# The first modulation's columns as TensorE products in four column groups, and the opening in a new written order

## The chip, the cores and the metric

The kernel runs on one core of a Trainium2 chip. The metric is device time in microseconds (us), the median of several executions. One execution is profiled as well. Engines are named as in the profile: PE is TensorE's matmul row and PEld its weight loads, DVE is VectorE, ACT is ScalarE, POOL is GpSimd, SP is SyncE, which issues most of the DMAs.

## The reference

One layer of a diffusion backbone over 1024 latent tokens of 1024 channels, with 256 context tokens. What matters here is its beginning: a conditioning vector gives six modulation vectors by one matrix product, the first two of which shift and scale the normed tokens, and the tokens then go through one wide input projection.

```
c_silu = silu(c);  cctx_silu = silu(c_ctx)
sh1, sc1, g1, sh2, sc2, g2 = split(c_silu @ w_ada + b_ada, 6)
csh1, csc1, ...            = split(cctx_silu @ w_ada + b_ada, 6)
hx = rmsnorm(x, norm1_g)   * (1 + sc1)  + sh1
hc = rmsnorm(ctx, norm1_g) * (1 + csc1) + csh1
xq, xk, xv, ... = split(hx @ w_in, offsets)
cq, ck, cv, ... = split(hc @ w_in, offsets)
```

Neighbourhood attention, retention, a merge, and a gated MLP with a depthwise convolution follow. Neither kernel differs from the other in those.

## The kernel before

Tokens are held transposed: channels on the 128 partitions, in eight channel blocks kb of 128, tokens along the free axis, in halves of 512 for the latent grid and one piece of 256 for the context. Each 32-bit product is made of three products of a high part and a low part (`mm3`, L123 to L125; `chain`, L112 to L114): high with high, high with low, low with high. The high part is a rounded copy made on ACT, the low part what is left, subtracted on DVE.

The opening is one block of code under a manual schedule: the order in which the lines are written is the order of each engine's instructions, and each engine takes its own in that order. SP's queue of loads is ordered in the same way, and a load whose buffer is still read holds all loads behind it. The opening's steps are small functions:

- `load_x`, `square_x`, `rstd_x`, `scale_x` (L161, L164, L168 and L169, L172): a block of 128 token rows (eight of the grid, tb 0 to 7, two of the context, 8 and 9) is loaded, squared with a sum on ACT, its root taken on POOL, and its rows scaled on DVE.
- `transp` (L199): PE turns a 128x128 piece of a scaled block into a PSUM bank; eight for each block, 80 in all. The banks have three tags, tp, c0 and c1, with two, three and three buffers, which are all eight banks. `evac_t` (L207) copies a full bank to SBUF on ACT or DVE; where it isn't called, the modulation reads the bank.
- `mod_h` (L219) on ACT gives the modulated high part, `mod_v` (L223) on DVE the same in full precision, `mod_l` (L228) on DVE the low part. `ctx_h`, `ctx_v`, `ctx_l` are the same for the context.
- `load_first`, `split_hi`, `split_lo` (L325, L328): the first pair's q, k, v weights and their two parts. `first_mm(half, kb)`: nine products of 512 columns that add channel block kb to q, k and v of one half of the tokens; sixteen calls in all.
- The shift and scale columns come in two ways. For channel blocks 0 to 3 (`NPE = 2` groups of two blocks), `ag_mm` (L265) multiplies on PE: the vector piece of 128 channels is the stationary operand, 32 columns wide, and 512 weight columns stream; four pieces go to four groups of 32 columns of the array, and add up in four strips of one bank. `ag_ev` copies the bank, `ag_tr` (L274) sums the strips and turns them into columns with four small products, `ag_fin` (L280, L281) adds the bias on DVE. For channel blocks 4 to 7 the weights come transposed and the vector is spread over all partitions (`load_bc`, `silu_bc`, cs0 for the latent tokens, cs1 for the context): `ada_stt` (L303) multiplies and sums on DVE, or `ada_prod` (L309) multiplies on POOL and `ada_sum` (L313) sums on ACT; `ada_fin` (L298, L299) adds the bias.
- Row blocks and modulation weights share one tag, `x`, of 14 buffers of 512 KB.

Then the first pair's q, k and v are copied out of PSUM (`ev_hi`, `ev_lo`), the next pair's q weights (`next_load`, `next_hi`, `next_lo`, L592 and L595) are split, and `next_mm` (L112 to L114) and `ctx_mm` run on PE beside it; `decays` (L556 to L561) makes small tables for the retention on ACT. Behind the manual part a scheduler orders the attention of four pairs, with projections as filler work.

Of the kernel before, what the change touches and what calls it, by code (L numbers as in the profile page):

```python
# [16 lines left out]
P = 128  # L17
# [16 lines left out]
NPE = 2  # L34
# [6 lines left out]
def tile_hybrid_layer(ctx, tc: tile.TileContext, io, dbg=None):  # L41
# [112 lines left out]
    xs, xT = {}, {}  # L154
# [39 lines left out]
    def transp(tb, kbs, tags=None):  # L194
        grid, half, i = tb < NTB, tb // 4 % 2 if tb < NTB else 0, tb % 4 if tb < NTB else tb - NTB
        for n, kb in enumerate(kbs):
            if i == 0:
                tps[grid, half, kb] = p_tile(tags[n])
            pe.transpose(tps[grid, half, kb][:, i * P : (i + 1) * P], xs[tb][:, kb * P : (kb + 1) * P], ident)  # L199
# [4 lines left out]
    def evac_t(grid, half, kb, eng):  # L204
        moved.add((grid, half, kb))
        x = xT[grid, kb, half]
        copy[eng](x, tps[grid, half, kb][:, : x.shape[-1]])  # L207


    def turned(grid, half, kb):  # L210
        x = xT[grid, kb, half]
        return x if (grid, half, kb) in moved else tps[grid, half, kb][:, : x.shape[-1]]
# [22 lines left out]
    cs2 = [(s0 if i else csp).tile([P, D], F32, name=f"cs{i}") for i in range(2)]  # L235
    wad = {}
# [9 lines left out]
    def load_bc(i):  # L246
        sync.dma_start(cs2[i], io["cvec"][i : i + 1].to_broadcast([P, D]))

    def silu_bc(i):
        act.activation(cs2[i], cs2[i], AF.Silu)  # L250


    ag, arow, arow_s, acolT = {}, {}, {}, {}

    def load_ag(g, q):
        ag[g, q] = s_tile("x", 14)
        sync.dma_start(ag[g, q], io["w_ada1g"][g, q])

    def ag_mm(g, q):
        if q == 0:  # L260
            arow[g] = p_tile("tp")
        for e in range(2):
            k = 2 * q + e
            c = 32 * (k % 4)
            pe.matmul(arow[g][c : c + 32], ccol[:, k], ag[g, q][:, e * 512 : e * 512 + 512], start=k < 4, stop=k >= 4)  # L265
# [5 lines left out]
    def ag_tr(g):  # L271
        acolT[g] = p_tile("tp")
        for n in range(4):
            pe.matmul(acolT[g][:, 2 * n : 2 * n + 2], arow_s[g][:, n * P : n * P + P], csum, start=True, stop=True)  # L274

    def ag_fin(g):
# [3 lines left out]
        vec.tensor_tensor(t, acolT[g][:, 0:8].rearrange("p (i k s) -> p i k s", i=2, k=2), bb[:, :, kbs].unsqueeze(3).to_broadcast([P, 2, 2, 2]), ALU.add)  # L280
# [4 lines left out]

    def load_ada(kb):
        wad[kb] = [s_tile("x", 14) for _ in range(2)]
        for i in range(2):
            sync.dma_start(wad[kb][i], io["w_ada1"][kb - 2 * NPE, i])


    acol = cpool.tile([P, 2, KB, 2], F32, name="acol")

    def ada_fin(kb, s, eng):
        t = acol[:, s, kb]
        eng = pool if eng == "pool" else vec
        bb = cst["b"][:, 0:16].rearrange("p (i k) -> p i k", i=2)
        eng.tensor_tensor(t, t, bb[:, :, kb], ALU.add)  # L298
        eng.tensor_tensor(t[:, 1:2], t[:, 1:2], cst["g"][:, 0, kb : kb + 1], ALU.mult)  # L299
        (ca if s else cx)[kb] = (t[:, 1:2], t[:, 0:1])  # L300

    def ada_stt(kb, s, i):
        vec.scalar_tensor_tensor(s_tile("aj", 1), wad[kb][i], 1.0, cs2[s], ALU.mult, ALU.mult, accum_out=acol[:, s, kb, i : i + 1])  # L303

    prods = {}

    def ada_prod(kb, s, i):
        prods[kb, s, i] = s_tile("prod", 3)
        pool.tensor_tensor(prods[kb, s, i], wad[kb][i], cs2[s], ALU.mult)  # L309

    def ada_sum(kb, s, i):
        t = prods[kb, s, i]
        act.activation(t, t, AF.Copy, accum_out=acol[:, s, kb, i : i + 1])  # L313
# [6 lines left out]
    def load_first(half):  # L320
        for t in range(3):
            fraw[half, t] = rawload(io["w_qkv"][0, t, half])
# [7 lines left out]
    def first_mm(half, kb):  # L330
        xh, xl = hxs(0, half)(kb), hxs(1, half)(kb)
        if kb == 0:
            ch[half] = [p_tile(f"c{half}") for _ in range(3)]
        for t in range(3):
            wc, c0 = first[t][kb // 4], (kb % 4) * P
            mm3(perm(ch[half][t], 8), wc[:, 0, c0 : c0 + P], wc[:, 1, c0 : c0 + P], xh, xl, kb == 0, kb == KB - 1)
# [202 lines left out]
    def ada_col2(i):  # L539
        w = ada2[i]  # L540
        late(vec.scalar_tensor_tensor(w, w, 1.0, cs2[0], ALU.mult, ALU.mult, accum_out=col[:, 16 + i : 17 + i]))
        if i + 1 < 32:
            ada_load()
# [46 lines left out]
    def next_hi(i):  # L590
        nxt[i] = place if i else wtile()
        act.copy(nxt[i][:, 0], nraw[i])  # L592
# [21 lines left out]
    ch = {}  # L614
    with tc.manual_schedule():
        load_ag(0, 0)
        load_cc()
        load_x(0)
        load_x(1)
        silu_cc()  # L620
        square_x(0)
        rstd_x(0, 1)
        scale_x(0)
        ag_mm(0, 0)
        load_ag(0, 1)
        ag_mm(0, 1)
        transp(0, (2,), ("c0",))
        transp(0, (3,), ("c1",))
        load_x(2)
        load_ag(0, 2)  # L630
        transp(0, (7,), ("tp",))
        square_x(1)
        rstd_x(1, 1)
        load_cols()
        transp(0, (0,), ("c0",))
        transp(0, (4,), ("c1",))
        ag_mm(0, 2)
        load_x(3)
        load_ag(0, 3)
        scale_x(1)  # L640
        one_plus()
        transp(1, (2,), ("c0",))
        square_x(2)
        rstd_x(2, 1)
        scale_x(2)
        transp(1, (7,), ("tp",))
        transp(0, (1,), ("c0",))
        transp(1, (1,), ("c0",))
        transp(0, (5,), ("c1",))
        transp(2, (1,), ("c0",))  # L650
        load_ag(1, 1)
        load_ag(1, 0)
        square_x(3)
        rstd_x(3, 1)
        scale_x(3)
        transp(1, (0,), ("c0",))
        transp(2, (7,), ("tp",))
        transp(1, (4,), ("c1",))
        transp(2, (2,), ("c0",))
        transp(2, (4,), ("c1",))  # L660
        ag_mm(0, 3)
        transp(3, (1,), ("c0",))
        transp(3, (4,), ("c1",))
        transp(1, (5,), ("c1",))
        transp(2, (5,), ("c1",))
        transp(2, (0,), ("c0",))
        transp(3, (5,), ("c1",))
        load_first(0)
        load_ag(1, 2)
        transp(3, (2,), ("c0",))  # L670
        transp(1, (3,), ("c1",))
        transp(3, (7,), ("tp",))
        ag_ev(0, "act")
        ag_tr(0)
        ag_fin(0)
        transp(3, (0,), ("c0",))
        mod_h(True, 0, 0)
        mod_v(True, 0, 0)
        split_hi(0, 0)
        evac_t(True, 0, 7, "act")  # L680
        ag_mm(1, 0)
        ag_mm(1, 1)
        transp(2, (3,), ("c1",))
        transp(3, (3,), ("c1",))
        transp(0, (6,), ("tp",))
        transp(1, (6,), ("tp",))
        transp(2, (6,), ("tp",))
        load_ag(1, 3)
        mod_l(True, 0, 0)
        split_hi(0, 2)  # L690
        split_lo(0, 2)
        evac_t(True, 0, 5, "vec")
        load_x(4)
        ag_mm(1, 2)
        transp(3, (6,), ("tp",))
        ag_mm(1, 3)
        evac_t(True, 0, 4, "act")
        split_hi(0, 1)
        split_lo(0, 0)
        mod_h(True, 0, 1)  # L700
        evac_t(True, 0, 2, "act")
        load_x(5)
        load_x(6)
        square_x(4)
        mod_v(True, 0, 1)
        mod_l(True, 0, 1)
        evac_t(True, 0, 6, "vec")
        split_lo(0, 1)
        first_mm(0, 0)
# [1439 lines left out]
```

## Time and profile before

| | us |
|---|---|
| median of 3 runs | 1754.88 (1753.91 to 1762.69) |
| the profiled execution | 1755.57 |
| its span, first to last instruction | 1753.8 |
| PE busy in the span | 1707.4 (97%) |
| DVE busy | 1318.1 (75%) |
| ACT busy | 846.3 (48%) |
| POOL busy | 542.6 (31%) |
| mean granted clock of PE | 0.992 |

The span is cut into 40 slices on the page; each digit is a busy share in tenths:

```profile
PE   7799999999999999999999999999999999999997
DVE  5978888766677776787664557888999899866655
POOL 2600000003333343055413300244555555111444
PEclk9899999999999999999999999999999999999998
```

The first slice is 44 us long, and so is the second. They hold the opening: PE is below nine tenths there, DVE at nine in the second slice, POOL busy and then idle for long. A busy share is read with care, since matmuls are pipelined.

### The profile page before, as it was taken

How to read it: one execution, taken by the hardware profiler on the slowest of the kernel's cores; microseconds unless marked ns; L12 is line 12 of the kernel's file. 1: busy time of each engine (PE TensorE's matmuls, PEld its weight loads, DVE VectorE, ACT ScalarE, POOL GpSimd, SP SyncE). 2: the span in 40 equal slices, each digit the busy share in tenths (PEclk: the TensorE clock that was granted, in tenths of full speed). 3: DMA queues.
4: the chain of work that ended last, by engine and by line, in shares of the span. 5: the costliest groups of instructions: out<-in, count | busy, mean ns of one | idle time of the engine just before them, and what ended most of it. 6: DMA issues, size and time to landing. Idle time of an engine off the chain costs nothing.

```text
span 1753.8 us, 24617 instructions
## 1 busy us (share of the span) xinstructions
PE 1707.4 (97%) x8270; PEld 1416.1 (81%) x8270; DVE 1318.1 (75%) x2510; ACT 846.3 (48%) x1802; POOL 542.6 (31%) x459
## 2 busy tenths in 40 slices
PE   7799999999999999999999999999999999999997
PEld 4588888888888888888888888878888888888886
DVE  5978888766677776787664557888999899866655
ACT  6666666653343434543344323634444444554443
POOL 2600000003333343055413300244555555111444
PEclk9899999999999999999999999999999999999998
DMA  9143334442342322677668643723223332586753
GB/s 373 45 123 126 106 105 143 135 146 85 92 130 77 103 62 87 191 243 244 202 195 303 217 154 133 266 86 118 91 90 112 117 103 90 184 286 194 243 171 147
DMA packets 158143, 268.20 MB, mean 153 GB/s; under 512 B 26080, under 2 KB 46784, under 8 KB 158016
## 3 DMA queue, kind: packets, MB, share of 16 engines
q1 hardware_dynamic: 140096, 245.65, 42.7%
q10 hardware_dynamic: 17920, 20.98, 3.4%
q8 instruction: 65, 1.06, 0.3%
q14 instruction: 62, 0.51, 0.1%
HBM read 192.32 MB, written 71.61 MB: 150 GB/s over the span
## 4 chain that ended last, share of the span: by engine, by line
PE 38%; issue 7%; DVE 6%; DMA 3%; POOL 3%; ACT 2%; SPq 0%; ACTq 0%; POOLq 0%; DVEq 0%
PE u L1414 23%; PE y L1414 4%; PE pr L114 2%; PE pr L112 2%; PE pr L113 2%; PE om L125 1%; PE om L124 1%; PE om L123 1%; DVE wc L1440 1%; DMA raw<-d_orr 1%; PE pn L114 1%; PE pn L112 1%; PE pn L113 1%; DMA uu<-d_t 1%; DMA vo<-d_h 1%
## 5 line engine op out<-in xcount | busy, mean ns | idle before, releaser
L1414 PE MATMUL u<-T,wc 128*128 128x512 f32 x960 | 227.5, 393 | 3.8 <-ACT pu L1460 2.6
L1414 PEld LDWEIGHTS u<-T,wc 128*128 128x128 f32 x960 | 180.5, 189 | 45.1 <-ACT pu L1460 6.3
L1414 PE MATMUL y<-wc,ahl 128*128 128x512 f32 x924 | 212.2, 392 | 2.0 <-DVE wc L89 1.8
L1414 PEld LDWEIGHTS y<-wc,ahl 128*128 128x128 f32 x924 | 174.5, 189 | 39.4 <-DVE wc L89 2.5
L113 PE MATMUL mm<-low,wc 128*128 128x512 f32 (+1 forms) x328 | 124.5, 380 | 0.0
L1414 PE MATMUL u<-h2a,wc 128*128 128x512 f32 x480 | 112.4, 390 | 0.7 <-DVE pu L1469 0.7
L112 PE MATMUL mm<-hx,wc 128*128 128x512 f32 x264 | 107.0, 405 | 0.3 <-DVE vc L223 0.3
L89 DVE TENSOR_TENSOR wc<-ur,wc 128x512 fp32r<-128x512 f32 x77 | 60.8, 793 | 61.1 <-ACT wc L88 61.1
L1414 PEld LDWEIGHTS u<-h2a,wc 128*128 128x128 f32 x480 | 90.0, 188 | 19.9 <-DVE pu L1469 1.2
L114 PE MATMUL mm<-hx,wc 128*128 128x512 f32 x264 | 106.0, 402 | 0.0
L1439 ACT CAST wc<-s 128x512 fp32r<-128x512 f32 x80 | 49.6, 622 | 91.0 <-PE u L1414 87.1
L125 PE MATMUL mm<-wc,low 128*128 128x512 f32 (+1 forms) x240 | 91.4, 381 | 0.0
L1414 PE MATMUL u<-hxT,wc 128*128 128x512 f32 x384 | 90.1, 390 | 0.6 <-DVE pu L1469 0.6
L1566 POOL TENSOR_TENSOR col<-col,bcol 128x32 f32<-128x32 f32 x1 | 0.2, 250 | 278.1 <-DVE st L486 278.1
L1440 DVE TENSOR_TENSOR wc<-s,wc 128x512 fp32r<-128x512 f32 x80 | 82.9, 1037 | 3.7 <-ACT wc L1439 3.4
L88 ACT CAST wc<-ur 128x512 fp32r<-128x512 f32 x77 | 47.7, 620 | 77.9 <-PE y L1414 73.0
L1414 PEld LDWEIGHTS u<-hxT,wc 128*128 128x128 f32 x384 | 71.9, 188 | 16.4 <-issue 1.6
L89 DVE TENSOR_TENSOR wc<-raw,wc 128x512 fp32r<-128x512 f32 x93 | 63.2, 687 | 19.3 <-ACT wc L88 18.8
L88 ACT CAST wc<-raw 128x512 fp32r<-128x512 f32 x93 | 57.2, 620 | 39.5 <-DMA raw<-in_w_pret 7.6
L123 PE MATMUL mm<-wc,hx 128*128 128x512 f32 x192 | 75.3, 392 | 0.6 <-ACT r L1115 0.6
L124 PE MATMUL mm<-wc,hx 128*128 128x512 f32 x192 | 75.2, 392 | 0.0
L1440 DVE TENSOR_TENSOR wc<-wr,wc 128x512 fp32r<-128x512 f32 x55 | 55.6, 1018 | 19.0 <-ACT wc L1439 17.0
(400 smaller groups left out, 4755.7 us busy)
## 6 DMA issues: line engine op xcount, KB each, us to landing
ur<-in_w_up SPq DMA_DIRECT2D x80, 256.0 KB
ur<-d_a SPq DMA_DIRECT2D x77, 256.0 KB
aw<-in_w_ada SPq DMA_DIRECT2D x32, 512.0 KB
pj<-in_w_down SPq DMA_DIRECT2D x44, 256.0 KB
d_w<-pj SPq DMA_DIRECT2D x44, 256.0 KB
d_a<-sa SPq DMA_DIRECT2D x44, 256.0 KB
ur<-d_w SPq DMA_DIRECT2D x44, 256.0 KB
d_a<-at SPq DMA_DIRECT2D x33, 256.0 KB
```

Of the source, the lines that this page charges most:

```text
L88: act.copy(hi, src)
L89: (lo_eng or vec).tensor_tensor(lo, src, hi.bitcast(F32), ALU.subtract)
L112: pe.matmul(out, wh, xh, start=k == 0, stop=False)
L113: pe.matmul(out, wh, xl, start=False, stop=False)
L114: pe.matmul(out, wl, xh, start=False, stop=k == n - 1)
L123: pe.matmul(out, ah, bh, start=first, stop=False)
L124: pe.matmul(out, ah, bl, start=False, stop=False)
L125: pe.matmul(out, al, bh, start=False, stop=last)
L1414: pe.matmul(out, a, b, start=first and n == 0, stop=last and n == 2, skip_group_check=True)
L1439: pin(act.copy(w[:, 0], a))
L1440: pin(vec.tensor_tensor(w[:, 1], a, w[:, 0].bitcast(F32), ALU.subtract))
L1566: pool.tensor_tensor(col[:, 16:48], col[:, 16:48], bcol[:, 16:48], ALU.add)
```

## The change

`NPE` goes from 2 to 4: all eight channel blocks get their columns from PE, and `ada_stt`, `ada_prod`, `ada_sum`, `ada_fin`, cs1 and the transposed weights are gone. cs0, which the second modulation still needs later, is loaded and put through silu at the end of the opening. `ag_mm` is called for four channel pieces at once, so all four column groups of the array run side by side, and the order in which its two halves come is free; the strips are summed into the same bank that held them.

```diff
-NPE = 2
+NPE = 4
...
-    def ag_mm(g, q):
-        if q == 0:
-            arow[g] = p_tile("tp")
-        for e in range(2):
-            k = 2 * q + e
-            c = 32 * (k % 4)
-            pe.matmul(arow[g][c : c + 32], ccol[:, k], ag[g, q][:, e * 512 : e * 512 + 512], start=k < 4, stop=k >= 4)
+    def ag_mm(g, r, tag):
+        first = g not in arow
+        if first:
+            arow[g] = p_tile(tag)
+        for k in range(4 * r, 4 * r + 4):
+            c, w = 32 * (k % 4), ag[g, k // 2][:, k % 2 * 512 : k % 2 * 512 + 512]
+            pe.matmul(arow[g][c : c + 32], ccol[:, k], w, start=first, stop=not first)
...
-    def ada_stt(kb, s, i):
-        vec.scalar_tensor_tensor(s_tile("aj", 1), wad[kb][i], 1.0, cs2[s], ALU.mult, ALU.mult, accum_out=acol[:, s, kb, i : i + 1])
...
-    def ada_prod(kb, s, i):
-        prods[kb, s, i] = s_tile("prod", 3)
-        pool.tensor_tensor(prods[kb, s, i], wad[kb][i], cs2[s], ALU.mult)
-
-    def ada_sum(kb, s, i):
-        t = prods[kb, s, i]
-        act.activation(t, t, AF.Copy, accum_out=acol[:, s, kb, i : i + 1])
```

The tag `x` has 19 buffers instead of 14. Two context pieces share one PSUM bank, each bank is filled in any order of blocks, and every piece is copied out by `evac_t` before it is modulated. `first_mm` may take channel blocks in any order. The next pair's first q weight goes to a place in the attention's own memory (`nxt`, which lies where PT will be) instead of a wc buffer.

```diff
-        xs[tb] = s_tile("x", 14)
+        xs[tb] = s_tile("x", NX)
...
+    def bank(grid, half, kb):
+        return (grid, half, kb if grid else kb // 2)
...
-        nxt[i] = place if i else wtile()
+        nxt[i] = place if i else first_next
```

The written order of the opening, some 300 lines, is new. Its last part reads:

```diff
+        first_mm(1, 3)
         next_load(0)
...
+        next_load(1)
+        load_bc()
+        load_ex()
+        silu_bc()
+        for h in range(RH):
+            decays(h)
         dec_scale()
...
+        next_hi(0)
+        next_lo(0)
+        next_hi(1)
+        next_lo(1)
         pairs.append(Pair(0))
         ev_hi(1, 0, 0)
```

Three places show what moves. The first is the start of SP's queue, before the change: `in_x` and `in_ctx` are token rows, `in_w_ada1g` the modulation weights for PE, `ccol` the conditioning vectors.

```order
L257 DMA x<-in_w_ada1g 128x1024
L240 DMA ccol<-in_ccol 128x8x2
L161 DMA x<-in_x 128x1024 x2
L257 DMA x<-in_w_ada1g 128x1024
L161 DMA x<-in_x 128x1024
L257 DMA x<-in_w_ada1g 128x1024
L74 DMA bcol<-in_bcol 128x48
```

And with the change:

```order
L161 DMA x<-in_x 128x1024
L161 DMA x<-in_ctx 128x1024
L161 DMA x<-in_x 128x1024 x3
L161 DMA x<-in_ctx 128x1024
L161 DMA x<-in_x 128x1024 x4
L247 DMA ccol<-in_ccol 128x8x2
L265 DMA x<-in_w_ada1g 128x1024 x4
L93 DMA raw<-in_w_qkv 128x512
L265 DMA x<-in_w_ada1g 128x1024
```

All ten blocks of token rows, the context's two among them, now stand ahead of the vectors and of every weight.

The second place is PE up to its first product for q, k and v, which is the first row of L123; `ident` is a transpose, `ccol` a modulation product, `csum` a sum of strips. Before:

```order
L199 MATMUL tp<-ident,x 128x128
L274 MATMUL tp<-csum,arow 128x2 x4
L199 MATMUL c_204<-ident,x 128x128
L265 MATMUL tp<-x,ccol 32x512 x4
L199 MATMUL c_188<-ident,x 128x128 x2
L199 MATMUL tp<-ident,x 128x128 x3
L265 MATMUL tp<-x,ccol 32x512 x2
L199 MATMUL tp<-ident,x 128x128
L265 MATMUL tp<-x,ccol 32x512 x2
L123 MATMUL c_319<-hx_123,wc 128x8x8x8
```

And with the change:

```order
L203 MATMUL c_376<-ident,x 128x128 x3
L203 MATMUL c_327<-ident,x 128x128
L273 MATMUL tp<-x,ccol 32x512 x4
L203 MATMUL tp<-ident,x 128x128 x2
L273 MATMUL tp<-x,ccol 32x512 x4
L281 MATMUL tp<-csum,arow 128x2 x4
L203 MATMUL c_322<-ident,x 128x128
L123 MATMUL c_461<-hx_123,wc 128x8x8x8
```

Before, 32 of the 80 transposes and the sums of group 0 alone stood ahead of that product; now all 80 transposes and the sums of group 1 do.

The third place is DVE in the middle of the opening: `vh` is a modulated piece, `low` a low part, `wc` a weight, `aj` a column sum. Before:

```order
L303 SCALAR_TENSOR_TENSOR aj,acol<-x,cs_152 128x1024
L228 TENSOR_TENSOR low<-vh,hx_129 128x512
L228 TENSOR_TENSOR low<-vh,hx_133 128x512
L223 TENSOR_SCALAR vh<-low,acol 128x512
L228 TENSOR_TENSOR low<-vh,hx_137 128x512
L223 TENSOR_SCALAR vh<-low,acol 128x512
L328 TENSOR_TENSOR wc<-raw,wc 128x512 x2
L228 TENSOR_TENSOR low<-vh,hx_107 128x512
L303 SCALAR_TENSOR_TENSOR aj,acol<-x,cs_152 128x1024
```

And with the change, from the columns of group 1 on:

```order
L287 TENSOR_TENSOR acol<-tp,bcol 128x2x2x2
L288 TENSOR_TENSOR acol<-acol,gcol 128x2x2
L231 TENSOR_SCALAR vh<-low,acol 128x512
L236 TENSOR_TENSOR low<-vh,hx_127 128x512
L231 TENSOR_SCALAR vh<-low,acol 128x512
L231 TENSOR_SCALAR vc<-low,acol 128x256
L236 TENSOR_TENSOR low<-vh,hx_129 128x512
L231 TENSOR_SCALAR vh<-low,acol 128x512 x2
L236 TENSOR_TENSOR low<-vh,hx_135 128x512
```

The column sums are gone from DVE, and the context's pieces (`vc`) stand among the grid's instead of at the end. Behind the opening the instructions of every engine are the same, in the same order.

More of the change, by code (lines that the diff above doesn't have):

```diff
@@ L192, in tile_hybrid_layer, with transp, turns @@
     tps = {}
[L194 to L199, printed above, removed]
+    def bank(grid, half, kb):
+        return (grid, half, kb if grid else kb // 2)
+    def transp(tb, kb, tag):
+        grid = tb < NTB
+        key = bank(grid, tb // 4 if grid else 0, kb)
+        if key not in tps:
+            tps[key] = p_tile(tag)
+        c0 = tb % 4 * P if grid else kb % 2 * C + (tb - NTB) * P
+        pe.transpose(tps[key][:, c0 : c0 + P], xs[tb][:, kb * P : (kb + 1) * P], ident)
+    def turns(grid, half, kb):
+        t = tps[bank(grid, half, kb)]
+        return t if grid else t[:, kb % 2 * C : kb % 2 * C + C]
     copy = {"act": act.copy, "vec": vec.tensor_copy}
@@ L234, in tile_hybrid_layer @@
     csum = s0.tile([P, 2], F32, name="csum")
-    cs2 = [(s0 if i else csp).tile([P, D], F32, name=f"cs{i}") for i in range(2)]
-    wad = {}
+    cs2 = csp.tile([P, D], F32, name="cs")
     def load_cc():
@@ L271, in ag_tr @@
     def ag_tr(g):
-        acolT[g] = p_tile("tp")
         for n in range(4):
-            pe.matmul(acolT[g][:, 2 * n : 2 * n + 2], arow_s[g][:, n * P : n * P + P], csum, start=True, stop=True)
+            pe.matmul(arow[g][:, 2 * n : 2 * n + 2], arow_s[g][:, n * P : n * P + P], csum, start=True, stop=True)
     def ag_fin(g):
@@ L318, in tile_hybrid_layer, with load_f @@
     fraw = {}
-    def load_first(half):
-        for t in range(3):
-            fraw[half, t] = rawload(io["w_qkv"][0, t, half])
+    def load_f(half, t):
+        fraw[half, t] = rawload(io["w_qkv"][0, t, half])
     def split_hi(half, t):
@@ new lines, in tile_hybrid_layer @@
+        evac_t(False, 0, 5, "act")
+        load_ag(0, 1)
+        transp(9, 1, "c0")
+        load_ag(0, 3)
+        silu_cc()
+        transp(8, 0, "c0")
+        square_x(4)
+        transp(3, 5, "c0")
+        transp(3, 2, "c1")
+        transp(3, 0, "tp")
+        transp(2, 4, "c1")
+        transp(0, 1, "c0")
+        load_f(0, 1)
+        rstd_x(4, 1)
+        transp(8, 7, "c1")
+        transp(9, 0, "c0")
+        transp(8, 6, "c1")
+        transp(2, 1, "c0")
+        evac_t(True, 0, 3, "act")
@@ L917, in tile_hybrid_layer @@
-        ctx_l(5)
-        ctx_h(6)
-        ctx_l(6)
+        ag_tr(3)
+        split_lo(1, 2)
+        mod_h(True, 1, 4)
+        mod_l(True, 0, 5)
+        mod_h(True, 1, 5)
+        first_mm(0, 4)
+        ag_fin(3)
+        ctx_v(7)
+        ctx_h(7)
+        mod_v(True, 0, 7)
+        mod_v(True, 0, 6)
+        mod_v(True, 1, 7)
+        ctx_v(6)
+        mod_h(True, 0, 6)
+        ctx_l(7)
+        mod_h(True, 0, 7)
+        mod_l(True, 0, 6)
+        mod_l(True, 0, 7)
+        mod_h(True, 1, 7)
@@ new lines, in tile_hybrid_layer @@
+        first_mm(0, 5)
+        first_mm(0, 6)
+        mod_l(True, 1, 7)
+        mod_v(True, 1, 5)
+        mod_h(True, 1, 6)
+        ctx_v(5)
+        first_mm(0, 7)
+        mod_l(True, 1, 5)
+        mod_v(True, 1, 4)
+        ctx_h(6)
+        mod_v(True, 1, 6)
+        first_mm(1, 7)
+        ctx_l(5)
+        mod_l(True, 1, 6)
+        first_mm(1, 5)
+        first_mm(1, 1)
+        ctx_h(4)
+        mod_l(True, 1, 4)
+        ctx_l(6)
+        first_mm(1, 6)
+        first_mm(1, 4)
+        first_mm(1, 0)
@@ L2063, in layout @@
     out["ccol"] = ac(out["cvec"].reshape(2, KB, P).transpose(2, 1, 0))
-    out["w_ada1"] = ac(w_ada[:, :2048].T.reshape(2, KB, P, D).transpose(1, 0, 2, 3)[2 * NPE :])
     out["w_ada2"] = ac(w_ada[:, 2048:].T.reshape(32, P, D))
```

541 lines of the change are left out of this document (230 added, 311 removed).

## The prediction

> **What bounds the kernel now.** I read the page first, then the windows before and after the point where the change ends, then PE's and DVE's instructions in order of time. The columns of a window are its length, the busy time of PE, PEld, DVE, ACT and POOL with counts, the granted clock, the DMA share and GB/s.
>
> ```profile
> 0.00:84.19 84.19, 61.70 (x273) 42.43 (x273) 61.86 (x87) 52.66 (x105) 37.18 (x44) 0.92 0.57 214
> 84.19:1753.80 1669.61, 1645.69 (x7998) 1373.69 (x7998) 1256.24 (x2424) 793.67 (x1698) 505.42 (x416) 1.00 0.46 150
> ...
> 40.00:60.00 20.00, 14.78 (x54) 11.28 (x53) 18.81 (x19) 11.75 (x20) 14.95 (x13) 0.83 0.31 115
> 60.00:80.00 20.00, 13.14 (x52) 10.39 (x52) 19.53 (x29) 13.60 (x36) 10.67 (x6) 0.83 0.00 1
> ```
>
> At 84.19 us PE takes the first product of the next pair. From there PE is busy 98.6% of the time; before it, 73%. Between 40 and 80 DVE is the full engine (38.3 of 40 us), PE has 12 us free, and DMA is nearly idle from 60 on. So the opening waits for DVE, the rest for PE, and only the opening is edited.
>
> ```profile
> 48.67 0.79 PE L124 MATMUL c<-low,wc 128*128 128x512 f32 x1 [3.65 <-DVE low L228]
> ...
> 75.97 0.47 PE L199 MATMUL tp<-ident,x 128*128 128x128 f32 x1 [4.85 <-DVE vc L223]
> ...
> 84.19 0.47 PE L112 MATMUL mm<-hx,wc 128*128 128x512 f32 x1 [0.32 <-DVE vc L223]
> ...
> 95.77 0.36 PE L112 MATMUL mm<-hc,wc 128*128 128x256 f32 x1 [0.44 <-DVE qS L421]
> ```
>
> Every long wait of PE is for DVE. Why DVE is full is seen at one place: three POOL products and two row scalings of DVE begin together.
>
> ```profile
> 53.67 7.94 POOL L309 TENSOR_TENSOR prod<-x,cs 128x1024 f32<-128x1024 f32 x3
> ...
> 53.74 5.66 DVE L172 TENSOR_SCALAR x<-x,rstd 128x1024 f32<-128x1024 f32 x2 [0.86 <-POOL rstd L169]
> ...
> 29.30 0.74 DVE L172 TENSOR_SCALAR x<-x,rstd 128x1024 f32<-128x1024 f32 x1
> ```
>
> The scaling takes 0.74 us with POOL idle, and 2.83 us each beside the products. So the column sums on POOL cost DVE time too.
>
> **What goes.** The groups of instructions in the first 100 us name it:
>
> ```profile
> L309 POOL TENSOR_TENSOR prod<-x,cs 128x1024 f32<-128x1024 f32 x8 | 21.7, 2723 | 7.6 <-ACT prod L313 6.4 <-DMA x<-in_w_ada 1.1
> ...
> L303 DVE SCALAR_TENSOR_TENSOR aj<-x,cs 128x1024 f32<-128x1024 f32 x8 | 11.4, 1426 | 0.0
> ...
> L313 ACT ACTIVATE prod<-prod 128x1024 f32<-128x1024 f32 x8 | 8.4, 1055 | 0.9 <-POOL prod L309 0.9
> ```
>
> All three end: 11.4 us of DVE, 8.4 of ACT, 21.7 of POOL, with the stretching of DVE beside POOL. The weight bytes stay: eight 512 KB tiles for eight.
>
> **What comes, on PE.** Two more groups of four columns each.
>
> ```profile
> 16.98 1.09 PE L199 MATMUL c<-ident,x 128*128 128x128 f32 x8
> ...
> 19.23 1.07 PE L265 MATMUL tp<-x,ccol 128*32 128x512 f32 x8
> ...
> 27.44 0.95 PE L274 MATMUL tp<-csum,arow 128*128 128x2 f32 x8
> ...
> 79.72 0.39 PE L124 MATMUL c<-low,wc 128*128 128x512 f32 x1
> 79.94 0.39 PE L125 MATMUL c<-hx,wc 128*128 128x512 f32 x1
> ```
>
> Four products in four column groups (eight records) take 1.07 us, so a group's eight take 2.14, and its column sums 0.95: 3.1 us, twice. A product of 512 columns starts every 0.228 us, so one row block for q, k and v (nine) takes 2.05 us. Eight transposes take 1.09 us.
>
> **When the modulation can start.** All ten row blocks stand ahead of the first weights on SP, so arrival sets the beginning.
>
> ```profile
> 7.45 1.06 ACT L164 ACTIVATE v<-x 128x1024 f32<-128x1024 f32 x1 [0.61 <-DMA x<-in_x]
> ...
> 8.80 1.06 ACT L164 ACTIVATE v<-x 128x1024 f32<-128x1024 f32 x1 [0.20 <-DMA x<-in_x]
> ...
> 20.00:40.00 20.00, 18.19 (x98) 12.95 (x95) 17.10 (x28) 16.65 (x29) 5.25 (x5) 1.00 1.03 404
> ```
>
> 512 KB at 404 GB/s is 1.30 us; the squares that wait for blocks start 1.35 apart. Block 0, now behind one large tile and the small ccol, lands by 7.4; alone in front, a block lands between 4.6 and 6.1 (one or two steps less; I take 4.6, since ccol's many small pieces go too). Then by count: group 0, the 14th large tile, at 4.6 + 13 x 1.30 + 0.8 for ccol = 22.3; group 1, four more tiles, a 256 KB weight and two small loads, at 28.3; group 2 at 36.1; group 3 at 40.7. Before, weights came among the first blocks and blocks 4 to 9 late, so the modulation now starts later, and the part behind it must win that back. The buffers (19 for 14) don't hold SP: the 20th tile waits for block 1, whose last transpose is the 45th of 80, done long before that tile's turn at 30 us.
>
> ```profile
> 16.96 0.59 ACT L269 COPY arow<-tp 128x512 f32<-128x512 f32 x1 [1.74 <-PE tp L265]
> ...
> 24.00 0.50 PE L123 MATMUL c<-hx,wc 128*128 128x512 f32 x1
> ...
> 30.61 0.80 ACT L219 ACTIVATE hx<-low,acol 128x512 fp32r<-128x512 f32 x1
> ...
> 22.40 0.68 DVE L207 COPY low<-c 128x512 f32<-128x512 f32 x1
> ...
> 49.68 0.54 DVE L223 TENSOR_SCALAR vh<-low,acol 128x512 f32<-128x512 f32 x1
> ...
> 64.43 0.68 DVE L228 TENSOR_TENSOR low<-vh,hx 128x512 fp32r<-128x512 f32 x1
> ...
> 84.48 0.42 DVE L223 TENSOR_SCALAR vc<-low,acol 128x256 f32<-128x256 f32 x1
> ```
>
> On PE the first product for q, k, v (24.00 in before) now stands behind all 80 transposes and group 1. Up to group 0 the transposes hide behind the loads: 80 at 0.136 are 10.9 us of PE, in banks that DVE and ACT must empty, 24 copies where there were 12. Group 0 goes from 22.3 over its products (2.1), the copy on ACT (0.6), the sums (0.95) and two small DVE instructions (0.35), with 0.4 of hops, to columns at 26.7. On DVE three modulations (two of 512, one of 256), two subtractions, three copies and two weights' low parts follow: 2 x 0.54 + 0.42 + 0.68 + 0.42 + 3 x 0.68 + 2 x 0.68 = 6.0, so the third weight is ready at 32.7. On PE group 1 has landed at 28.3 and waits for a bank and its place till 29.8 for the second half of its products; copy and sums follow, to 32 or 33. Both say **32.7 for the first product**; I take 31.5 and 35 as bounds, the later one for the first block landing at 6.1 with a copy or two in the way.
>
> **From there PE sets the end.** 16 blocks x 2.05 = 32.8, groups 2 and 3 another 4.3 and their sums 1.9: 39.0 us, **to 71.7**. Does DVE keep up? Group 1's columns are ready at 33.3; from there to the last weight's low part, which the fifth block needs, its column holds eight modulations (0.54) and eight subtractions (0.68) of 512, three of each of 256 (0.42), three low parts (0.68) and two small ones: 14.7 us, or 13 as far as rows start before the last has ended. That is 46.3 to 48. PE comes there after 4 x 2.05 + 4.3 + 1.9 = 14.4 us, at 47.1. So nothing to 1 us is lost. The last eight blocks then take PE 16.4 us and DVE some 7, so DVE is done first. DVE's whole opening adds up to 46 us (10 x 0.74, 8 x 0.68 copies, 6 x 0.68 parts, 16 x 0.54, 16 x 0.68, 16 x 0.42 for the context, 3 us of small ones) where it was 61.86 busy.
>
> The weights of the next pair are what PE takes next. They moved behind all of ACT's modulations:
>
> ```profile
> 31.32 1.05 ACT L250 ACTIVATE cs<-cs 128x1024 f32<-128x1024 f32 x1
> ...
> 60.58 1.28 ACT L556 ACT_TABLE_LOAD   x1
> ...
> 77.85 0.60 ACT L592 CAST wc<-raw 128x512 fp32r<-128x512 f32 x1
> 78.36 0.29 ACT L556 ACTIVATE dec<-ex,lg 128x1 f32<-128x1 f32 x1
> 78.56 0.28 ACT L557 ACTIVATE dec<-ex,lg 128x1 f32<-128x1 f32 x1
> ```
>
> After ACT's last modulation (about 54 on DVE's count) come silu (1.05), the table (1.28), 24 decays 0.19 apart (4.6), two casts (1.2) and DVE's part (0.7): 62 to 64. PE arrives at 72, so 8 us cover it; all exposed it would cost its 8.8. Behind them the evacuations of the first pair queue; a cast for the pair after stands among them and waits for the last use of the first weights, so they mostly run beside the next pair's 11 us of products, as they do now.
>
> **Sum.** With 0.3 of hop and half a microsecond of stall, the next pair starts at 72.5 instead of 84.19: 11.7 less. The 0.44 stall at 95.77 should go, as half the evacuations come earlier: 12.1. Behind it the order is unchanged and PE-bound, so it carries. The profiled execution took 1755.57 (span 1753.8 and 1.77 around it), so 1743.5; the median shown is 0.69 lower, and I forecast **1743**. Bounds: first product 1.2 earlier or 2.3 later, DVE 0 to 4 short: 1740 to 1749.
>
> **Rivals.** *The clock is half at the start of the products.*
>
> ```profile
> 6.90 1.92 PE L265 MATMUL tp<-x,ccol 128*32 128x512 f32 x4 [6.90 <-ACT ccol L244]
> ...
> 15.86 1.05 PE L265 MATMUL tp<-x,ccol 128*32 128x512 f32 x4
> ...
> 48.00:52.00 4.00, 3.33 (x8) 2.66 (x9) 4.00 (x9) 1.51 (x3) 1.15 (x3) 0.51 0.41 133
> ...
> 50.97 0.63 PE L123 MATMUL c<-hx,wc 128*128 128x512 f32 x1
> 51.39 0.63 PE L124 MATMUL c<-low,wc 128*128 128x512 f32 x1
> ```
>
> After 3.65 us of idling the clock is 0.51 and products start 0.43 apart. The first group's four records took 1.92, later ones 1.05. PE now has nothing but transposes for its first 10 us. If they don't wake it, groups 0 and 1 take 2 us more in the chain and the first eight products 1.6: 4 us, 1747. For: the opening rows are slow. Against: between 11.9 and 15.9 transposes stood mixed with products and it woke. Chance 0.15. The Trainium skill, "TensorE: Matmul & The Clock Gate", Part 4: PE-mode transpose, states that transposes don't count as work for the gate; this trace, where the two are mixed, can't decide it.
>
> *DVE stays the bound.* If the searched order makes it wait for ACT at each block, PE goes at DVE's pace: 5 us lost, 1748. Chance 0.14.
>
> *The gain is taken back later*, by loads that now fall together: 1753 to 1755. Only 1.4% of PE's time behind 84.19 is idle. Chance 0.05.
>
> *Slower:* the clock stays half through the products. Each costs 0.20 more; the 12.1 are gone at 60 of the 144, and all 144 give +29, 1772. It needs gaps all along, as DVE made them before; there half clock ended after some 14 products each time. Chance 0.06.
>
> That the column sums stay on DVE is excluded by the order: no such row is left.
>
> **Chances.** Forecast 0.60 (1740 to 1746), the others as given. Within 0.5% (8.8 us, about what can be told from no change) fall two thirds of the first rival, most of the second, and the third: faster 0.71, same 0.23, slower 0.06. The range 1740 to 1749 leaves out the last two rivals.
>
> **What will show it.** Right: no 128x1024 product on POOL or DVE in the first 100 us; scalings all near 0.75; first q, k, v product near 33; next pair near 72 with PE full from 50. Wrong: a clock below 0.9 between 30 and 60 (first rival), waits of PE for low (second), a cast of the next pair as PE's last releaser (ACT's tail uncovered).

## The result, and the profile after

| | before | after |
|---|---|---|
| median of 7 runs each, us | 1755.21 (1752.28 to 1762.69) | 1741.64 (1737.7 to 1745.63) |
| ratio of the two | | 0.9915, 95% interval 0.9892 to 0.9938 |
| the profiled execution | 1755.57 | 1743.48 |
| its span | 1753.8 | 1741.4 |
| first q/k/v product starts | 24.00 | 35.48 |
| next pair's first product starts | 84.19 | 74.16 |
| first context product | 95.77 | 85.30 |

The change makes the kernel 0.85% faster. The windows of the kernel after, cut as those of before were (length, busy time of PE, PEld, DVE, ACT and POOL with counts, granted clock, DMA share, GB/s):

```profile
0.00:74.16 74.16, 57.11 (x320) 42.85 (x321) 46.39 (x94) 52.58 (x105) 16.21 (x33) 1.00 0.69 254
74.16:1741.40 1667.24, 1643.64 (x7999) 1371.83 (x7997) 1250.72 (x2412) 787.64 (x1687) 501.09 (x410) 1.00 0.46 149
40.00:60.00 20.00, 20.00 (x112) 14.59 (x105) 19.01 (x43) 18.11 (x41) 0.00 (x0) 1.00 0.50 172
60.00:80.00 20.00, 20.00 (x90) 16.57 (x89) 8.10 (x12) 9.42 (x22) 4.90 (x5) 1.00 0.27 79
```

Between 40 and 80 us the full engine has changed: PE is busy 40 of 40 us at full clock, where it had 27.9. DVE's busy time up to the next pair has shrunk from 61.86 to 46.39 us. Behind the opening PE is as busy as before (98.6%).

PE's instructions of the opening in order of time (start, length, and in brackets what ended an idle time), the first q/k/v product being L123 and the next pair's L112:

```profile
10.59 0.47 PE L203 MATMUL c<-ident,x 128*128 128x128 f32 x1 [10.59 <-DVE x L172]
14.41 1.76 PE L203 MATMUL c<-ident,x 128*128 128x128 f32 x7 [3.35 <-DVE x L172]
...
19.87 1.15 PE L203 MATMUL c<-ident,x 128*128 128x128 f32 x9
...
22.70 1.06 PE L203 MATMUL c<-ident,x 128*128 128x128 f32 x8 [1.46 <-DVE low L215]
...
24.56 1.92 PE L273 MATMUL tp<-x,ccol 128*32 128x512 f32 x16 [0.25 <-ACT low L215]
...
27.25 0.55 PE L203 MATMUL c<-ident,x 128*128 128x128 f32 x3 [0.51 <-DVE x L172]
...
28.41 0.95 PE L281 MATMUL tp<-csum,arow 128*128 128x2 f32 x8
...
35.48 0.47 PE L123 MATMUL c<-hx,wc 128*128 128x512 f32 x1
...
74.16 0.39 PE L112 MATMUL mm<-hx,nxt 128*128 128x512 f32 x1
...
85.30 0.36 PE L112 MATMUL mm<-hc,wc 128*128 128x256 f32 x1
```

From 35.48 to 74.16 no wait is left. Ahead of it there are two things that the forecast did not have: the transposes from 14.41 to 19.2 us start 0.21 us apart and only then 0.11, and the sums of group 0 (28.41) stand behind transposes that wait for a scaling (27.25). Where that scaling comes from is seen on ACT:

```profile
20.62 0.65 ACT L215 COPY low<-c 128x256 f32<-128x256 f32 x2 [2.87 <-PE c L203]
21.28 1.28 ACT L251 ACT_TABLE_LOAD   x1
22.58 0.42 ACT L251 ACTIVATE ccol<-ccol 128x256 f32<-128x256 f32 x1
22.90 1.04 ACT L164 ACTIVATE v<-x 128x1024 f32<-128x1024 f32 x1
...
54.46 1.05 ACT L257 ACTIVATE cs<-cs 128x1024 f32<-128x1024 f32 x1
55.51 1.28 ACT L535 ACT_TABLE_LOAD   x1
...
61.27 0.60 ACT L571 CAST nxt<-raw 128x512 fp32r<-128x512 f32 x1
```

Block 4's square (22.90) waits in ACT's queue behind copies, the sigmoid table and the SiLU. Its root on POOL follows, block 7's root stands behind that in POOL's queue, and the scalings of blocks 4 and 7 on DVE come last:

```profile
24.98 0.75 DVE L172 TENSOR_SCALAR x<-x,rstd 128x1024 f32<-128x1024 f32 x1 [0.70 <-POOL rstd L169]
26.45 0.75 DVE L172 TENSOR_SCALAR x<-x,rstd 128x1024 f32<-128x1024 f32 x1 [0.71 <-DMA bcol<-in_bcol]
...
29.45 0.17 DVE L287 TENSOR_TENSOR acol<-tp,bcol 128x8 f32<-128x8 f32 x1 [0.92 <-PE tp L281]
29.66 0.17 DVE L288 TENSOR_TENSOR acol<-acol,gcol 128x4 f32<-128x4 f32 x1
```

The columns of group 0 are complete at 29.83. The scaling at 26.45 is put down to a DMA; POOL's root for block 7 is written from 25.86 to 26.41 and fits that start as well.

### The profile page after: what moved, and what is told of

It reads as the page before. It is cut to its first block, busy times and chain, and to the rows that moved or that the text cites. A ratio compares the mean times of both kernels' runs of the same rounds, so it can differ in the third digit from the quotient of the medians.

```text
span 1741.4 us, 24675 instructions
## 1 busy us (share of the span) xinstructions
PE 1700.8 (98%) x8318; PEld 1414.7 (81%) x8318; DVE 1297.1 (74%) x2505; ACT 840.2 (48%) x1791; POOL 517.3 (30%) x443
## 4 chain that ended last, share of the span: by engine, by line
PE 76%; issue 7%; DVE 6%; POOL 4%; DMA 3%; ACT 3%; SPq 0%; POOLq 0%; ACTq 0%; DVEq 0%
PE u L1387 26%; PE y L1387 4%; PE mm L114 4%; PE mm L112 4%; PE mm L113 4%; PE mm L123 3%; PE mm L124 3%; PE mm L125 3%; PE R L496 2%; PE pr L112 2%; PE ptp L478 2%; PE pr L113 2%; PE pr L114 2%; PE om L125 1%; PE om L123 1%
## 5 line engine op out<-in xcount | busy, mean ns | idle before, releaser
L112 PE MATMUL mm<-hx,wc 128*128 128x512 f32 x256 | 103.7, 405 | 0.0
L114 PE MATMUL mm<-hx,wc 128*128 128x512 f32 x256 | 102.8, 402 | 0.0
L123 PE MATMUL mm<-wc,hx 128*128 128x512 f32 x192 | 75.2, 392 | 0.6 <-ACT r L1088 0.6
```

What stands on the lines that cost most here:

```text
L112: pe.matmul(out, wh, xh, start=k == 0, stop=False)
L114: pe.matmul(out, wl, xh, start=False, stop=k == n - 1)
L123: pe.matmul(out, ah, bh, start=first, stop=False)
```

## The experiments

Totals of one kernel spread by some 8 us, which is more than half of the change's own gain, so the opening is judged by its marks: first transpose, first q/k/v product, next pair's first product. The first transpose itself comes between 10.0 and 11.0 us from one execution to the next, so the distance from it is the cleaner number.

| kernel | first transpose | first q/k/v product | distance | next pair | ratio of medians to before, run beside it, 95% interval |
|---|---|---|---|---|---|
| after | 10.59 | 35.48 | 24.89 | 74.16 | 0.9915 (0.9892 to 0.9938) |
| `e1_clear_first` | 10.61 | 35.87 | 25.26 | 74.55 | 0.9903 (0.9887 to 0.9920) |
| `e_nx14` | 10.05 | 35.33 | 25.28 | 74.01 | 0.9915 (0.9896 to 0.9935) |
| `e_warm` | 10.17 | 35.14 | 24.97 | 73.81 | 0.9916 (0.9903 to 0.9928) |
| `e1c_sq4` | 12.06 | 35.80 | 23.74 | 74.48 | 0.9920 (0.9901 to 0.9938) |
| `e_sq4` | 10.94 | 34.54 | 23.60 | 73.22 | 0.9883 (0.9867 to 0.9900) |
| `e_warm_sq4` | 10.96 | 33.13 | 22.17 | 71.81 | 0.9912 (0.9894 to 0.9930) |

The first four have the same chain of work up to the first product apart from one part, and their distances lie within 0.4 us. `e_tail4` and `e_pin_after` below, whose chain up to there is that of the kernel after, have 25.57 and 25.23, so differences of up to 0.7 us mean nothing.

### What the parts of the change are worth

**Columns on PE, old order.** The kernel before with `NPE = 4`; groups 2 and 3 stand where the old order had its sums, and all `ada_` steps are gone.

```diff
-NPE = 2
+NPE = 4
...
-        ada_sum(4, 0, 1)
+        ag_mm(2, 0)
+        ag_mm(2, 1)
...
+        ag_ev(2, "act")
+        ag_tr(2)
+        ag_fin(2)
```

> The kernel before, with all columns as products on PE (NPE = 4) and its old written order: the DVE and POOL column sums are taken out and groups 2 and 3 put where the old order had a first sum and a third block's products. If the columns carry the gain, the first product stays near 24 us, DVE's rows are short everywhere, and PE's first product for the next pair comes at 70 to 76 us (84.19 before, 74.16 with the whole change): 1741 to 1747. If the new order carries it, that product stays at 80 or later: 1751 or more.

Measured: next pair at 80.54, 3.65 us earlier, where the whole change gives 10.03. Median 1745.33, ratio 0.9933 (0.9915 to 0.9951). By the mark, this order keeps about a third of the opening's gain. The totals don't separate this kernel from the one after, since the two intervals overlap; they are taken up below. DVE is no longer full, but the chain of group 3 stands open, as DVE's instructions in order of time show:

```profile
52.06 0.17 DVE L280 TENSOR_TENSOR acol<-tp,bcol 128x8 f32<-128x8 f32 x1 [8.33 <-PE tp L274]
...
55.26 0.69 DVE L228 TENSOR_TENSOR low<-vh,hx 128x512 fp32r<-128x512 f32 x1
```

DVE stands idle for 8.33 us until the sums are there, PE then waits 2.59 us for the low part, and from 50 to 60 us it is busy for 6.04 us at a clock of 0.71. Where the two groups stand was my choice, so this is one old order and not the best one: that a new order was needed at all isn't shown.

**POOL's share alone.** The kernel before with POOL's eight column products and ACT's eight sums done as eight more sums on DVE.

```diff
-        ada_prod(6, 0, 0)
-        ada_sum(6, 0, 0)
+        ada_stt(6, 0, 0)
```

> The kernel before, with the eight column products of POOL (and their sums on ACT) done as eight more sums on DVE. If POOL's products stretch DVE's work by some 14 us, as the rows of before suggest (two scalings in 5.66 us, a low part in 2.63), then DVE pays 8 x 1.2 = 9.8 and saves 14, and the next pair starts near 80 instead of 84.19: 1751. If DVE pays nothing for POOL, DVE has 9.8 us more and the next pair starts near 94: 1765.

The two groups of DVE in the first 90 us (busy time, mean ns of one):

```profile
L303 DVE SCALAR_TENSOR_TENSOR aj<-x,cs 128x1024 f32<-128x1024 f32 x16 | 19.5, 1220 | 0.2
...
L172 DVE TENSOR_SCALAR x<-x,rstd 128x1024 f32<-128x1024 f32 x10 | 7.3, 751 | 13.0 <-POOL rstd L169 13.0
```

DVE's sums grew from 11.4 to 19.5 us, and still its busy time up to the next pair fell from 61.86 to 55.98 and the next pair came at 76.27 instead of 84.19. So POOL's products had cost DVE 14 us (5.9 less plus 8.1 of new sums). Taking them off POOL, and their sums off ACT, moves the next pair by 7.9 us in the old order, where 4 were expected and the whole change gives 10.03. A wait of 1.79 us for DVE then stands ahead of the first context product; the median is 1750.85, ratio 0.996 (0.9943 to 0.9977).

### Why the first product comes at 35.5 and not at 32.7

**The loads.** SyncE waits for POOL's memset of `ccol` before it can issue that load (15.71 us) and the weights behind it (16.44). Here the memset stands first.

```diff
+    def clear_cc():
+        pool.memset(ccol, 0.0)
+
     def load_cc():
-        pool.memset(ccol, 0.0)
...
     with tc.manual_schedule():
+        clear_cc()
         load_x(1)
```

> The changed kernel, with POOL's clearing of ccol moved to the head of POOL's queue, so that SP doesn't wait for it with the loads of all modulation weights (issued at 15.71 us in the changed kernel, after SP had nothing from 6.3 on). If these loads set the first product, it comes at 32.5 to 33 instead of 35.48 and the next pair at 71 to 72 instead of 74.16: 3 us less. If the chain over ACT and POOL sets it (the copies of context pieces at 20.62, the table load, the square of block 4 at 22.90, its root), the first product stays after 34.5.

`ccol` was issued at 7.70 and the weights from 8.96, over 7 us earlier, and nothing moved: distance 25.26. The theory that these loads alone set the first product fell. Fewer buffers point the same way:

```diff
-    xs, xT, NX = {}, {}, 19
+    xs, xT, NX = {}, {}, 14
```

> Kernel after with 14 buffers for row blocks and weights of the modulation instead of 19 (the kernel before had 14 in two pools). Computes the same. The 15th tile (a tile of group 1's weights) then waits until the first row block's last transpose is read, at about 23 us, instead of being issued at about 17. Theory 'the buffers are needed for group 1': group 1's products move from 31.31 to about 33 to 35, the first q/k/v product from 35.48 to 37 to 39, the next pair's first product from 74.16 to 76 to 78, total 2 to 4 us more. Rival 'the loads don't set the opening' (clearing ccol first had brought them 8 us forward and changed nothing): first product and total the same within 0.5 us.

Distance 25.28, next pair at 74.01: the five more buffers of the change are not needed for its gain.

**The half rate of the transposes.** 84 transposes of the identity keep PE busy ahead of the real ones.

```diff
+    wake = p_tile("tp")
+
+    def stir(n):
+        for _ in range(n):
+            pe.transpose(wake[:, 0:P], ident, ident)
...
+        stir(60)
         transp(0, 2, "c1")
+        stir(24)
```

> Kernel after, with 84 transposes of the identity into an unused PSUM tile on TensorE: 60 ahead of the first real transpose and 24 behind it, so that TensorE is busy from about 1.5 us to 14.4 us, where in kernel after it waits. Computes the same. Question: is the late first q/k/v product (35.48 us against the 32.7 forecast) due to the transposes of 14.41 to 19.5 us, which ran at half rate (0.21 us apart instead of 0.11)? Theory 'cold transposes': the real transposes from 14.4 on are 0.11 us apart, about 2.5 us are saved on TensorE's queue, group 0's columns are ready at 27.5 instead of 29.83, the first q/k/v product starts at 33 to 33.5, the next pair's first product at 71.7 to 72.2 instead of 74.16, total 2 to 2.5 us less. Rival 'scalings and copies': TensorE only waits longer for VectorE's scalings and copies; first product 35.0 to 35.5, next pair's first product 73.7 to 74.2, total the same.

Distance 24.97: no change. But the run does not test its theory cleanly, since the clock fell again; PE's instructions and windows show it:

```profile
1.36 8.97 PE L597 MATMUL tp<-ident 128*128 128x128 f32 x60 [1.36 <-POOL ident masks.py:199]
10.17 0.31 PE L203 MATMUL c<-ident,x 128*128 128x128 f32 x1
10.31 2.78 PE L597 MATMUL tp<-ident 128*128 128x128 f32 x24
13.97 0.99 PE L203 MATMUL c<-ident,x 128*128 128x128 f32 x7 [0.87 <-DVE x L172]
15.84 0.33 PE L203 MATMUL tp<-ident,x 128*128 128x128 f32 x1 [0.88 <-DVE x L172]
```

```profile
16.00:19.00 3.00, 3.00 (x16) 2.77 (x16) 2.14 (x6) 1.15 (x2) 1.59 (x3) 0.53 0.72 147
```

The first seven transposes ran at full rate (0.99 us where they had taken 1.76); after two pauses of 0.87 and 0.88 us the clock was 0.53 from 16 to 19 us, and the gain was gone.

**The square of block 4,** first with `ccol` loaded and its SiLU done ahead of everything, so that ACT has no table to load among the copies:

```diff
+        load_cc()
         load_x(1)
+        silu_cc()
         square_x(1)
...
         square_x(7)
+        square_x(4)
...
-        load_cc()
...
-        silu_cc()
...
-        square_x(4)
```

> The changed kernel, with ccol cleared, loaded and put through silu first, and the square of block 4 right behind that of block 7. It frees the loads as the run with the clearing alone does, and also the chain over ACT and POOL. If either of the two sets the first product, it comes at 31.5 to 33 here, and the next pair at 70.5 to 72: 2 to 4 us less than the changed kernel. If neither, it stays at 35.

`ccol` in front delayed all row blocks by 1.5 us (first transpose 12.06), so the first product moved to 35.80; from the first transpose on, 1.15 us were won. Without that load in front, block 4 ahead of block 7 and the memset first:

```diff
+        clear_cc()
         load_x(1)
...
+        square_x(4)
         square_x(7)
...
-        square_x(4)
```

> Kernel after with ccol's clearing at the head of GpSimd's queue and block 4's square ahead of block 7's, and no transposes of the identity: the run with both (first q/k/v product 33.13 us, next pair's first product 71.81) without its first part. Computes the same. Question: which of the two brought the 2.35 us? Theory 'the squares chain': all of it comes from blocks 4 and 7 being scaled at 21.9 instead of 24.98 and 26.45; TensorE's half rate on the transposes is hidden behind the scalings; first q/k/v product 33.1 to 33.8, next pair's first product 71.8 to 72.5. Rival 'both are needed': the transposes at half rate hold the groups' products back by another 1 to 2 us; first product 34.3 to 35.5, next pair's first product 73 to 74.2.

Distance 23.60, 1.3 us less than after, next pair at 73.22. The rival held: this is one half. The scalings of blocks 4 and 7 now follow each other without a wait, and the transposes are still at half rate:

```profile
14.77 1.76 PE L203 MATMUL c<-ident,x 128*128 128x128 f32 x7 [3.35 <-DVE x L172]
...
24.53 1.41 DVE L172 TENSOR_SCALAR x<-x,rstd 128x1024 f32<-128x1024 f32 x2
```

The memset stands first in this run and in the next, so how much the square would have given with the late loads isn't measured. With the transposes of the identity added:

> Kernel after, with the 84 transposes of the identity of the run before, ccol's clearing at the head of GpSimd's queue (so that SyncE doesn't wait for it), and block 4's square ahead of block 7's on ScalarE instead of behind the sigmoid table and the SiLU (22.90 us), so that blocks 4 and 7 are scaled as soon as VectorE comes to them instead of at 24.98 and 26.45. Computes the same. Theory 'three small chains, each hidden behind the others': alone each gives nothing, together the sums of group 0 no longer wait for block 7's transposes, group 0's columns at 26 to 27, first q/k/v product 31.5 to 33, next pair's first product 70.5 to 72, total 2.5 to 3.5 us less than kernel after. Rival 'the copies set it' (ScalarE's and VectorE's copies of the turned blocks, about 12 us of work on each between 18 and 35): first product not before 35, total as kernel after.

```profile
10.96 0.27 PE L203 MATMUL c<-ident,x 128*128 128x128 f32 x1
11.07 2.78 PE L599 MATMUL tp<-ident 128*128 128x128 f32 x24
13.87 0.99 PE L203 MATMUL c<-ident,x 128*128 128x128 f32 x7
15.72 0.33 PE L203 MATMUL tp<-ident,x 128*128 128x128 f32 x1 [0.86 <-DVE x L172]
...
23.17 1.93 PE L275 MATMUL tp<-x,ccol 128*32 128x512 f32 x16
...
33.13 0.47 PE L123 MATMUL c<-hx,wc 128*128 128x512 f32 x1
```

Here only one such pause fell, the clock stayed full, and the real transposes came 0.11 us apart until they ran into the copies. Distance 22.17, another 1.4 us. The two causes together are 2.7 us. The pair with one more wait far behind the opening, below, repeats it: 25.23 in `e_pin_after`, 22.46 in `e_pin_warm_sq4`. The total did not follow: 2.5 to 3.5 us less than the kernel after was expected, and the ratio is 0.9912 against 0.9915.

### The tail on ACT

Each of the 24 exponentials of the decay tables is done four times, 13.4 us more on ACT (72 more, 0.186 apart).

```diff
-        for h in range(RH):
+        for h in list(range(RH)) * 4:
             decays(h)
```

> Kernel after with each of the decay tables' exponentials on ScalarE done four times (24 become 96, each about 0.19 us: some 13.7 us more on ScalarE; the result is the same). Question: what covers the tail that ScalarE has ahead of the next pair's first product? Theory of the prediction (it ends at 63.2, TensorE is full to 74.16: 11 us of cover): casts of the next weights end at about 75.5 and VectorE's low half at 77, so the next pair's first product starts at 76.5 to 78 instead of 74.16, total 2 to 4 us more. Rival 'the tail is on the path': 13 us more on both. Rival 'there is more cover than that' (the next pair's weights are not what that product waits for): 74.2 and no change.

```profile
76.80 0.50 PE L112 MATMUL mm<-hx,nxt 128*128 128x512 f32 x1 [1.48 <-ACT nxt L571]
```

PE's wait is 1.48 us and is put down to the cast of the next pair's weight: the tail was covered by some 12 us (13.4 less 1.48; this is one execution). In the kernel after that cast ended at 61.87, 12.3 us ahead of 74.16. Most of the rest of the 2.64 us by which this mark moved was there at the first product already (36.50 instead of 35.48).

### Why the totals spread

In this part the kernels are unchanged. Between 1100 and 1150 us the profiles differ by some 5 us, and it is one meeting of DVE and POOL. The kernel after, in order of time:

```profile
1125.11 7.60 DVE L89 TENSOR_TENSOR T<-uu,T 128x512 fp32r<-128x512 f32 x7
...
1125.42 1.53 POOL L1402 TENSOR_TENSOR s<-s,ur 128x512 f32<-128x512 f32 x1 [10.54 <-DMA ur<-in_w_up]
...
1126.91 1.75 POOL L1403 TENSOR_TENSOR s<-ur 128x512 f32<-128x512 f32 x1
...
1128.73 1.62 POOL L1404 TENSOR_TENSOR s<-ur,s 128x512 f32<-128x512 f32 x1
```

and `e_nx14`:

```profile
1123.31 4.29 DVE L89 TENSOR_TENSOR T<-uu,T 128x512 fp32r<-128x512 f32 x7
...
1123.56 5.20 POOL L1402 TENSOR_TENSOR s<-s,ur 128x512 f32<-128x512 f32 x1 [10.25 <-DMA ur<-in_w_up]
```

Either three of DVE's low halves take 1.78 us each instead of 0.68, as long as POOL's sums beside them, or POOL's sum waits until DVE's run has ended. In the first case the conv steps behind DVE's run are late and PE stands:

```profile
1120.00:1140.00 20.00, 16.79 (x71) 13.22 (x70) 19.86 (x22) 12.26 (x20) 4.86 (x3) 0.97 0.48 158
1140.00:1150.00 10.00, 10.00 (x41) 8.14 (x40) 7.54 (x8) 2.03 (x4) 9.31 (x6) 0.89 0.41 153
```

(kernel after: 3.2 us idle, then a clock of 0.89), against `e_nx14`:

```profile
1120.00:1140.00 20.00, 19.98 (x89) 16.22 (x88) 19.83 (x24) 11.67 (x19) 13.71 (x6) 1.00 0.52 168
```

Of the eleven profiles without a further edit there, six show the first case (both kernels of the comparison among them) and five the second. The old order with columns on PE had the second, and its offset to before jumps by 5.0 us between 1127 and 1182 us. So of the 13.7 us by which its profile is shorter, 3.65 were there at the next pair and 5.0 come from this meeting; the other 5 built up in small steps on both sides of it and stay unexplained. Which case its three other executions had isn't known, so its median stays open. To take the meeting away, POOL's sum of that unit waits for DVE's last low half; both engines keep their order.

```diff
-            own(eng.tensor_tensor(self.s2, self.s1, self.a11, ALU.subtract))
+            behind(own(eng.tensor_tensor(self.s2, self.s1, self.a11, ALU.subtract)))
...
+        low_of = last_vec()
         conv(j, *us2)
-    units[PLAIN + 1].load()
+    units[PLAIN + 1].load(behind=lambda ins: after_vec(ins, low_of))
```

> Kernel before, with one wait added far behind the opening, at about 1130 us: GpSimd's second sum of the second up-projection unit waits for the last of VectorE's 10 low halves of the combined operand T (both engines keep their order). Computes the same. Question: is the spread of 5 us and more between executions of one kernel the meeting of these two? In the runs so far VectorE's run of seven low halves took 7.6 us and TensorE then stood for 3 to 4 us, or 4.3 us and GpSimd's sum 5.2 in its place, by chance. Theory 'the meeting': the run of low halves takes 4.3 us each time, TensorE is busy over 19.5 of 20 us there, the median falls by 3 to 5 us to 1751 to 1754 and the spread to under 4 us. Rival 'the stall is of the loads': no change, 1755 to 1759 with a spread of 8.

> Kernel after, with the same wait at about 1130 us as in the run before this. Computes the same. Theory 'the meeting': median 1737 to 1740 with a spread under 4 us; against the kernel before with the same wait, a difference of 11 to 13 us, which is then the change's own. Rival 'the stall is of the loads': 1741 to 1746 with a spread of 8.

Measured: 1753.78 (1752.21 to 1755.41) for before, 1740.87 (1738.15 to 1742.18) for after, spreads of 3.2 and 4.0 us where the kernel before alone had 7.1 beside them (1753.07 to 1760.21). The low halves took 0.69 us each in both, and before gained 3.6 us on the median of its unpinned runs. So for the kernel before the meeting held as a cause. After came out above the 1737 to 1740 expected, and hardly below its 1741.64 without the wait; PE still stands 0.4 and 0.65 us there, and spreads of 3 to 4 us are left in both. With the meeting gone in both, the change is worth 12.9 us (1753.78 less 1740.87).

> Kernel after, with the 84 transposes of the identity, ccol's clearing first, block 4's square ahead of block 7's, and the wait at about 1130 us. Computes the same. If the opening's 2.35 us (next pair's first product 71.81 instead of 74.16) are carried to the end: 1.5 to 2.5 us less than the run before this, about 1735 to 1738, below both kernels. If they are given back at waits behind the opening (in the run without the added wait, 1.7 of them were left at 300 us and 0.6 at 700): within 0.7 us of the run before this.

Measured 1741.16 (1739.02 to 1742.21): the 2.9 us that this opening wins over the kernel with the same wait (next pair at 71.96 against 74.84) were still 2.4 at 690 us, and gone at 899, in four stands of PE of 0.3 to 1 us between 750 and 900. For three of its weight loads there (2.3 us in all) the profile names no releaser. So the better opening isn't shown to make a faster kernel. `e_sq4` has the best median, 1737.73, ratio 0.9883 (0.9867 to 0.99), below both kernels; but its interval overlaps that of after, it won only 0.94 us by the next pair, and its profiled execution, of the second case above, is the slowest of its four, so how much of the rest is its own stays open.

## Why the prediction held, and where it was off

- **What bounded the opening:** right. DVE was the full engine, and POOL's products were a cost to DVE. The size was larger than read from two scalings: with POOL's products done on DVE instead, DVE was busy 5.9 us less in spite of 8.1 us more work.
- **From the first product PE sets the end:** right. 39.0 us of work were forecast and 0.8 for hop and stall; 38.68 measured in all, clock 1.00, no stall. So the next pair came 1.7 us late (74.16 for 72.5), though the first product came 2.8 late. DVE did keep up. That it was busy for 46.39 us where 46 were added up is luck in part: DVE made twelve copies of transposed pieces where the sum had eight, and also rows for the first and the next pair that the sum left out, while rows overlap.
- **First product at 32.7:** this is the term that was mis-sized. It came at 35.48, beyond the later bound of 35. The step was "up to group 0 the transposes hide behind the loads", which put the columns of group 0 at 26.7; they were complete at 29.83. The count of loads had missed that SyncE's queue waits for POOL's memset (weights from 16.44), but that was not what set it: brought over 7 us forward, the loads changed nothing. The runs put 1.3 us on block 4's square, which the written order has behind a table load on ACT, and 1.4 us on transposes at half rate; without both the first product came at 33.13 and the next pair at 71.81, where 32.7 and 72.5 were forecast.
- **First rival, clock half at the start:** half right. The transposes did run at half rate, but they woke the clock themselves before the first product of a group (0.11 us apart from 19.2 on), so the groups ran at full rate (1.92 us for sixteen records) and the rival's 4 us did not come. The Trainium skill, "TensorE: Matmul & The Clock Gate", Part 4: PE-mode transpose, says that transposes don't count as work for the gate. These runs disagree for 32-bit transposes: in `e_warm` nothing but transposes of the identity had run when their spacing went from 0.21 to 0.11 us, after 4.5 us, and in `e_warm_sq4` after 5.7.
- **DVE as the bound, and half clock through the products:** neither came. From 35.48 to 74.16 PE has no wait for a low half. For the second the prediction read that half clock in the kernel before ended after some 14 products each time; it was about 14, 7 and 6, which makes that rival still less likely.
- **ACT's tail covered by 8 us:** right, and the cover was 12.
- **The stall at 95.77 goes:** right (85.30, no wait).
- **The gain carries:** right for this change. At the next pair the two profiles differ by 10.03 us, at the first context product by 10.47, at 703 us by 10.6, at 1685 by 11.4. The missing 1.6 of the opening was made up by small differences behind it, which go either way from run to run, as the meeting at 1125 us shows. That the forecast of 1743 came so close to a median of 1741.64 is luck to that extent. That PE is busy behind the opening does not alone make a gain carry: `e_pin_warm_sq4` lost its 2.9 us by 900, and `e2_dve_sums` had 7.9 at the next pair and 3.6 left at 1182.
- **The range:** its lower end of 1740 lies below what its terms give, since a first product 1.2 us earlier makes 1741.8; the measured 1741.64 lies just below that.

## What to carry to other kernels

Judge an edit of one stage by marks inside the trace, measured from a common start, and not by totals, when the totals spread by more than the edit is worth. When a stage waits on several short chains at once, undoing one may show nothing; take them away together, and then one by one. Before moving a product to an idle POOL, look at what DVE's instructions beside it cost.

## What the runs showed of the hardware

- These instructions of POOL and DVE took turns rather than shared: DVE's low halves took 0.68 us alone and 1.78 beside POOL's sums of 1.53 to 1.75, or POOL's sum took 5.2 to 5.5 us, until DVE's run ended. The Trainium skill, "Trainium Architecture — The Big Picture", "What this means for kernel authors", calls the pair's shared port an exclusive lock; the trace agrees.
- Pauses far shorter than the 3.65 us of the kernel before can be followed by half clock: two of 0.87 and 0.88 us within 3 us were in `e_warm` (0.53). One of 0.86 in `e_warm_sq4`, one of 1.46 in the kernel after and one of 1.60 later in `e_warm` were not. What decides isn't shown.
- The granted clock of a window reads 1.00 at the start of the program although PE runs at half rate there (transposes 0.21 us apart from 14.41 to 19.2 in the kernel after); the spacing of the instructions shows it, the clock column, the third from the end, doesn't:

```profile
14.00:18.00 4.00, 3.47 (x15) 3.07 (x16) 2.52 (x5) 2.30 (x4) 3.58 (x7) 1.00 0.48 138
```
